# The last chunk of the modulation moved from the query stage of a hybrid attention/mLSTM step to the second half of its first group's output projection

## The chip, the cores and the metric

One core of a Trainium2 chip. The metric is the device time of one execution in microseconds; the kernel before has a median of 1595.44 us over three runs (1595.12 to 1597.05). Engines are named as in the profile: PE is TensorE, PEld its weight loads, DVE is VectorE, ACT is ScalarE, POOL is GpSimd, SP is SyncE, which here issues most DMAs.

## The reference, cut to what matters

One layer of a diffusion backbone for one prompt of 128 context tokens and one sample of 1024 latent tokens, width D = 1024, all in 32-bit floats:

```python
mods = silu(cond) @ w_ada + b_ada              # six chunks of 1024: sh1, sc1, g1, sh2, sc2, g2
h = rmsnorm(x, norm1_w) * (1 + sc1) + sh1
aq, ak, av, mq, mk, mv, mo, mg = split(h @ w_in)
attn_o = attention(rope(rmsnorm(aq)), keys, vals)       # 8 query heads, 2 key heads of 64
hm = mlstm(mq, mk, mv, gates(mg)) in both directions    # 4 heads of 128, chunks of 128
hm = rmsnorm(hm, mlstm_norm_w) * sigmoid(mo)
x = x + g1 * (concat(attn_o, hm) @ w_out)
h2 = rmsnorm(x, norm2_w) * (1 + sc2) + sh2
x = x + g2 * ((silu(h2 @ w_gate) * (h2 @ w_up)) @ w_down)   # d_ff = 2816
y = rmsnorm(x, final_norm_w)
```

The context tokens have a modulation of their own and see only themselves; the latent tokens also see the cached context keys and start their scans from given states. Outputs are y of both token groups, the new keys and values, and the final mLSTM states of the context.

## The kernel before, in words

**Tiles.** The 1152 tokens are nine blocks of 128 (block 0 is the context), in three groups of three blocks (CT = 384 tokens). A product in full precision is made of three matmuls of a high and a low part of each operand: high by high, low by high, high by low (L495 to L497 in the in-projection, L1189 to L1191 in the output projection, L1321 to L1323 in the gate and up products, L1155 to L1157 in the down product). A weight piece is loaded as 32-bit `raw`, ACT casts its high part (L152 `whi`) and DVE or POOL subtracts for the low part (`sub`, L137 `wlo`). `Scaled.pairs` (L211) does this for the scaled 16-bit pieces of the in- and output projection: by default every second piece takes one ACT step (L221) and one DVE step (L222), the others two ACT steps (L224, L225) and a DVE subtraction.

**Order of stages.** (1) Loads, the first norm, key/value/gate products and the first two chunks of the modulation. (2) The query stage: 216 query matmuls (`linear_tok` with `evac_q`), and woven in with them `gates` (the mLSTM's gate algebra), `ada` (modulation), `kwork` (norm and rotation of the keys, key stacks, values) and `steps` (the weights of head 0). (3) Four mLSTM heads: each head's projections with the scan of the head before and attention of group 0 woven in. (4) The transition: scan of head 3, output projection of group 0 (`first_out`), second norm of group 0. (5) FFN of groups 0, 1, 2, with attention and output projection of the next group woven in.

**Modulation.** `ada_rest(ns, ...)` (L422) makes the chunks named in `ns` in units of one 512 KB load of w_ada (L428, tile `a`) and four strip products (L346, which the trace shows as eight records). After four units ACT copies `part` (L446); for chunks 3 and 4 (shift and scale) PE turns it into columns (L352), for chunks 2 and 5 (the two gates) PE makes a row (L455), which is stored in `g_d` (L459). Before, `ada` makes (2, 4, 3, 5) in the query stage: 32 units in all, with three `a` buffers.

**Queries.** `evac_q` scales a block's queries out of PSUM into `qraw`, and after a pair of blocks `norm_rope` (L672) norms and rotates them and SP stores them in `q_d` (L743), from where attention loads them.

**What sets the order.** Work is written as generators. `weave(main, side, n_main, n_side)` steps `side` about n_side times over n_main steps of `main`; `beside((gen, rate), ...)` steps several generators, each by its rate; `emit` runs one to its end. `hot(n)` raises the priority of what is issued inside. From program order, priority and dependencies a scheduler then fixes each engine's queue at build time; on the chip each engine serves its own queue strictly in order. SP's queue holds loads and stores in one order, so a load behind a store waits for what that store waits for. Tiles come from pools with a fixed number of buffers per tag, and a load into a tile waits for the last reader of the buffer.

**The transition.** `first_out` (L1198) loads the rows `x1a` and the gate rows, then for each block does the attention half of the output projection (`block(0, i)`: L1218 on DVE scales the product, L1219 on POOL adds it), makes the pieces of the second half of w_out (`homes`, `spare` and `iw`), and after the mLSTM's last head does `block(1, i)` for the three blocks (addition on DVE). Then `stats` (L1280) takes the squares of the three rows on ACT (L1284) and the inverse root for all three as a chain of 12 small DVE steps (L127 to L133), the rows are copied to `cur["x1"]` by DMA (L1452), and `norm2` (L1288) per block and half scales (L1300 `y`), transposes (L116), shifts and scales (L1308, L1310 `fl`), casts (L1315 `aTh`) and subtracts (L137 `aTl`, on POOL for group 0). Attention of group 1 (scores L1075, softmax L1077 to L1082, DMA transposes L1084 and L1085, value products L1099 and L1100) is already woven in with the last scan and with norm2. Then come the first gate and up products (`gate_up`, L1325), with two `raw` buffers.

```python
weave(linear_tok(w_q, 0, 512, evac_q(qp, qcc, qss, qw)),
      beside((gates, 0.7), (ada, 1.5), (kwork, 0.6), (steps, 0.3)), 40, 40)
...
att = chain(att, attention(1, oT, set()))
weave(scan, beside((first, 0.8), (att, 0.14)), 37, 37)
```

## Time and profile before

| | us |
|---|---|
| median of three runs | 1595.44 (1595.12 to 1597.05) |
| the profiled execution | 1595.83 |
| its span | 1593.8 |
| stage of loads, key/value/gate products | 0 to 92.7 |
| query stage | 92.7 to 185.1 |
| four heads | 185.1 to 485.5 |
| transition | 485.5 to 595.4 |
| FFN of group 0, 1, 2 | 595.4 to 960, to 1320, to 1593.8 |

The stage bounds are read from the PE timeline: the first product of head 0 starts at 185.07, the last in-projection product ends at 485.5, the first gate matmul starts at 595.45. The span is the time between the first and the last recorded instruction; the execution's own time is 2.0 us longer. In the lines of the profile an instruction group is given as engine, line of the program, operation, output<-inputs, partitions x elements and a count (x24); a bracket at the end holds the idle time of the engine before it and what ended it. A line number such as L346 is that of the kernel before, printed above; helpers such as `transpose` (L116) or `sub` (L137) have one line for all their callers, so the tile names tell them apart. The granted clock is the share of TensorE's full speed that the throttle allowed.

### The profile page before, as it was taken

What the parts mean: (1) busy time and instruction counts of PE and PEld (TensorE: products, weight loads), DVE (VectorE), ACT (ScalarE), POOL (GpSimd) and SP (SyncE); (2) the same over time, 40 slices, a digit from 0 to 9 for tenths busy, and PEclk for the clock granted to TensorE, in tenths of its full rate; (3) what the DMA queues carried; (4) which work ended last, traced back from release to release, by engine and by line L of the source; (5) the groups of instructions that cost most, each with busy time, mean ns of one, the idle gap of its engine ahead of it and who ended that gap; (6) DMA issues with size and microseconds to landing.
All of it is one profiled execution on the core that took longest, in us unless ns stands there. A gap on an engine that the chain in (4) does not pass through costs nothing.

```text
span 1593.8 us, 23426 instructions
## 1 busy us (share of the span) xinstructions
PE 1494.4 (94%) x8545; PEld 1217.9 (76%) x8545; DVE 1028.1 (65%) x2047; ACT 777.6 (49%) x1448; POOL 240.9 (15%) x341
## 2 busy tenths in 40 slices
PE   6899799999997859999999999999999999999996
PEld 3544467666674549899995989989895989999995
DVE  4877624755746966878637577887856575554555
ACT  4753446846655655555331545556541443333332
POOL 0213232323233221010010101000010101001111
PEclk9899699999999889999999999999999999999998
DMA  9565503522452357978634547978763545434441
GB/s 361 179 188 181 164 11 68 114 57 64 97 130 84 67 165 182 201 159 200 180 108 119 153 138 240 192 170 179 173 152 99 151 128 183 150 124 139 146 145 53
DMA packets 384888, 230.74 MB, mean 145 GB/s; under 512 B 169894, under 2 KB 346486, under 8 KB 384774
## 3 DMA queue, kind: packets, MB, share of 16 engines
q1 hardware_dynamic: 382118, 225.68, 53.3%
q10 hardware_dynamic: 2656, 3.58, 1.0%
q8 instruction: 67, 1.10, 0.3%
q14 instruction: 47, 0.39, 0.1%
HBM read 179.39 MB, written 9.92 MB: 119 GB/s over the span
## 4 chain that ended last, share of the span: by engine, by line
PE 58%; DVE 3%; DMA 1%; ACT 0%; issue 0%; ACTq 0%
PE mm L1322 12%; PE mm L1323 12%; PE mm L1321 11%; PE mm L1155 5%; PE mm L1156 5%; PE mm L1157 4%; PE S L1075 3%; PE po L1100 1%; PE po L1099 1%; PE mm L1189 1%; PE mm L1190 1%; PE mm L1191 1%; DVE fl L1310 1%; DVE x L1145 1%; DMA plT<-pl 1%; DVE wlo L137 0%
## 5 line engine op out<-in xcount | busy, mean ns | idle before, releaser
L152 ACT CAST whi<-raw 128x1024 fp32r<-128x1024 f32 (+1 forms) x204 | 209.0, 1025 | 375.6 <-PE mm L1322 151.5
L1321 PE MATMUL mm<-aTh,whi 128*128 128x384 f32 x1056 | 354.7, 337 | 5.0 <-ACT whi L152 5.0
L1322 PE MATMUL mm<-aTl,whi 128*128 128x384 f32 x1056 | 355.8, 337 | 2.7 <-DVE aTl L137 2.7
L137 DVE TENSOR_TENSOR wlo<-raw,whi 128x1024 fp32r<-128x1024 f32 (+1 forms) x204 | 245.4, 1203 | 171.4 <-ACT whi L152 168.8
L1323 PE MATMUL mm<-aTh,wlo 128*128 128x384 f32 x1056 | 354.9, 336 | 0.0
L137 POOL TENSOR_TENSOR hl<-tn,hl 128x384 fp32r<-128x384 f32 x66 | 82.6, 1252 | 884.9 <-ACT hl L1344 772.3
L1321 PEld LDWEIGHTS mm<-aTh,whi 128*128 128x128 f32 x1056 | 198.8, 188 | 6.0 <-ACT whi L152 5.4
L1322 PEld LDWEIGHTS mm<-aTl,whi 128*128 128x128 f32 x1056 | 198.9, 188 | 3.9 <-DVE aTl L137 3.3
L1323 PEld LDWEIGHTS mm<-aTh,wlo 128*128 128x128 f32 x1056 | 199.0, 188 | 0.1
L1156 PE MATMUL mm<-wlo,hl 128*128 128x512 f32 x372 | 145.4, 391 | 0.0
L1155 PE MATMUL mm<-whi,hl 128*128 128x512 f32 x372 | 144.7, 392 | 0.0
L1157 PE MATMUL mm<-whi,hl 128*128 128x512 f32 x372 | 143.1, 392 | 0.0
L495 PE MATMUL wi<-ipair,hT 128*128 128x384 f16 (+2 forms) x408 | 135.4, 334 | 1.9 <-ACT hT L519 1.2
L496 PE MATMUL wi<-ipair,hT 128*128 128x384 f16 (+2 forms) x408 | 135.3, 334 | 0.0
L497 PE MATMUL wi<-ipair,hT 128*128 128x384 f16 (+2 forms) x408 | 131.3, 333 | 1.0 <-DVE hT L137 1.0
L1082 DVE SCALAR_TENSOR_TENSOR pl<-pr,st,ph 128x1152 f16<-128x1152 f32 (+1 forms) x72 | 94.5, 1313 | 43.1 <-ACT ph L1081 36.5
L1078 ACT ACTIVATE pr<-S,st 128x1152 f32<-128x1152 f32 (+1 forms) x72 | 81.4, 1131 | 57.1 <-DVE st L1077 45.8
L1077 DVE TENSOR_REDUCE st<-S 128x1 f32<-128x1152 f32 (+1 forms) x72 | 88.7, 1233 | 19.0 <-PE S L1075 18.8
L1081 ACT ACTIVATE ph<-pr,st 128x1152 f16<-128x1152 f32 (+1 forms) x72 | 83.9, 1165 | 27.7 <-DVE st L1080 10.6
L1075 PE MATMUL S<-kst,qT 128*128 128x384 f32 (+1 forms) x400 | 88.8, 355 | 3.0 <-ACT pr L1078 2.8
L1157 PEld LDWEIGHTS mm<-whi,hl 128*128 128x128 f32 x372 | 69.9, 188 | 14.4
L1155 PEld LDWEIGHTS mm<-whi,hl 128*128 128x128 f32 x372 | 69.9, 188 | 13.8
(390 smaller groups left out, 2524.1 us busy)
## 6 DMA issues: line engine op xcount, KB each, us to landing
raw<-in_w_gu_dram SPq DMA_DIRECT2D x132, 512.0 KB, 4.1
raw<-in_w_down_dram SPq DMA_DIRECT2D x60, 512.0 KB, 4.1
a<-in_w_ada_dram SPq DMA_DIRECT2D x32, 512.0 KB, 4.5
gl<-g_d SPq DMA_DIRECT2D x34, 256.0 KB, 4.6
aw<-in_w_ada_dram SPq DMA_DIRECT2D x16, 512.0 KB, 10.1
iraw<-in_w_in_dram SPq DMA_DIRECT2D x32, 256.0 KB, 4.1
x<-in_x_sample_dram SPq DMA_DIRECT2D x14, 512.0 KB, 5.9
iraw<-in_w_out_dram SPq DMA_DIRECT2D x8, 512.0 KB, 5.1
```

The source lines that it names most:

```text
L137: (dve if eng == "dve" else pool).tensor_tensor(out=out, in0=full, in1=hi, op=ALU.subtract)
L152: nc.scalar.copy(hi[:, :n], raw[:, :n])
L495: mm(ps[:, :n], ah, wh[:, k % 2, c0 : c0 + n], start=(k == 0), stop=False)
L496: mm(ps[:, :n], ah, wl[:, k % 2, c0 : c0 + n], start=False, stop=False)
L497: mm(ps[:, :n], al, wh[:, k % 2, c0 : c0 + n], start=False, stop=(k == KD - 1))
L1075: mm(S[:, n, 0:w], qT[:, h, :], kst[kv][:, t, c0 + n * w : c0 + (n + 1) * w], start=(t == 0), stop=(t == 1))
L1155: mm(ps, ah, wh[:, k % 2, :], start=(k == 0), stop=False)
L1156: mm(ps, ah, wl[:, k % 2, :], start=False, stop=False)
L1157: mm(ps, al, wh[:, k % 2, :], start=False, stop=(k == nk - 1))
L1321: mm(ps, wh[:, k, :], th[:, k, :], start=(k == 0), stop=False)
L1322: mm(ps, wh[:, k, :], tl[:, k, :], start=False, stop=False)
L1323: mm(ps, wl[:, k, :], th[:, k, :], start=False, stop=(k == KD - 1))
```

## The change

- `ada` in the query stage makes chunks (2, 4, 3); chunk 5 (g2, eight units, two rows) becomes `ada5`, with a pool of its own (`a5` with two buffers), stepped beside the second output half and norm2 of group 0.
- The rates beside the query matmuls and beside the heads change: n_side 12 to 10 and `ada` 1.5 to 1.15, `att` 0.11 to 0.12, in the last scan `first` 0.8 to 0.5 and `att` 0.14 to 0.1.
- Query rows are stored one pair of blocks later (`late_q`, `flush_q`), the new key and value cache rows in `value_parts`.
- Both halves of w_out take the one-ACT, one-DVE form for every piece (`pairs(1)`).
- `first_out` ends after the pieces; the loop behind it does, for each block, the second output half with its sum written straight to `cur["x1"]`, that block's statistics, and norm2 of the block before. The three copies L1452 go. `aTl` is subtracted on DVE.
- Two gate pieces (`early`) are loaded before norm2 of the third block, attention of group 1 is set up only after `first_out`, and the PSUM pools of the FFN and the pool `hlp` open at other places.

```diff
@@ -461,7 +461,7 @@
 
     es_r = ExitStack()
     adp = es_r.enter_context(tc.tile_pool(name="adp", bufs=1, side="right", reuse_waits="tile"))
-    ada = ada_rest((2, 4, 3, 5), padded_sil(adp.tile([P, KD, 32], F32, name="silp2")),
+    ada = ada_rest((2, 4, 3), padded_sil(adp.tile([P, KD, 32], F32, name="silp2")),
                    lambda: adp.tile([P, 4, 256], F32, name=nm("a4"), tag="a4", bufs=3),
                    lambda: adp.tile([P, 512], F32, name=nm("part"), tag="part", bufs=1),
                    lambda: adp.tile([2, 512], F32, name=nm("row"), tag="row", bufs=1))
@@ -525,7 +525,7 @@
             features(c)
         prods = linear_tok(kvg_pairs, 0, 272, evac_kvg, (tuple(range(c * CB, c * CB + CB)),), bank if c == 1 else bankA)
         if c > 0:
-            weave(prods, chain(steps, ada), KD, 12)
+            weave(prods, chain(steps, ada), KD, 10)
         else:
             emit(prods)
         if c == 0:
@@ -705,8 +705,6 @@
         for b in (0, 4):
             norm_rope(qp, cc, ss, kall[:, b : b + 4], 4, NKV, kw, (b, b + 4))
             yield
-        dma(O["new_cache_k"][0, 0], kall[:, 9])
-        dma(O["new_cache_v"][0, 0], vall[:, 9])
 
         vm = qp.tile([P, 4], F32, name="vm")
         dve.tensor_reduce(out=vm[:, 0:1], in_=vall, axis=AX.XYZ, op=ALU.max, apply_absolute_value=True)
@@ -727,6 +725,13 @@
         dve.tensor_copy(vsc[:, 0:2], ps[:, 0:2])
         yield
 
+    late_q = []
+
+    def flush_q():
+        for bb, rows in late_q:
+            dma(q_d[bb], rows)
+        late_q.clear()
+
     def evac_q(qp, cc, ss, qw):
         held = {}
 
@@ -739,8 +744,8 @@
             if b == grp[-1]:
                 nb = len(grp)
                 norm_rope(qp, cc, ss, qr[:, 0:nb], nb, NQ, qw, (max(grp[0], 1) - 1, grp[-1]))
-                for i, bb in enumerate(grp):
-                    dma(q_d[bb], qr[:, i].rearrange("p h d -> p (h d)"))
+                flush_q()
+                late_q.extend((bb, qr[:, i].rearrange("p h d -> p (h d)")) for i, bb in enumerate(grp))
 
         return evac
 
@@ -936,7 +941,6 @@
                         continue
                     (nc.scalar.dma_start if h == NH - 1 and c > 0 else dma)(
                         hm_d[c][:, h * 2 * P : (h + 1) * 2 * P].rearrange("(b p) n -> p b n", p=P), t.rearrange("p b t x -> p b (t x)"))
-                    yield
             yield
 
 
@@ -996,6 +1000,9 @@
 
     def value_parts():
 
+        dma(O["new_cache_k"][0, 0], kall[:, 9])
+        dma(O["new_cache_v"][0, 0], vall[:, 9])
+        yield
         for i0 in (0, 5):
             v = vall[:, i0 : i0 + 5]
             dve.tensor_scalar(out=v, in0=v, scalar1=vsc[:, 0:1], scalar2=None, op0=ALU.mult)
@@ -1012,11 +1019,12 @@
     groups_in[0].inverses()
     steps = groups_in[1].ready()
     next(steps)
-    weave(linear_tok(w_q, 0, 512, evac_q(qp, qcc, qss, qw)), beside((gates, 0.7), (ada, 1.5), (kwork, 0.6), (steps, 0.3)), 40, 40)
+    weave(linear_tok(w_q, 0, 512, evac_q(qp, qcc, qss, qw)), beside((gates, 0.7), (ada, 1.15), (kwork, 0.6), (steps, 0.3)), 40, 40)
     emit(gates)
     emit(steps)
     groups_in[1].made = groups_in[1].pairs()
     emit(ada)
+    flush_q()
     emit(kwork)
     es_r.close()
     es_h.close()
@@ -1195,7 +1203,7 @@
         nc.scalar.copy(m[:, :, 0], o)
         sub(m[:, :, 1], o, m[:, :, 0], eng)
 
-    def first_out(oT, ready, mx, hm_done):
+    def first_out(oT, ready, mx, second):
 
 
         x1 = hTp.tile([P, CB, D], F32, name="x1a", tag="hT0")
@@ -1209,16 +1217,17 @@
             dma(x1[:, i], xrow(i))
         yield
 
-        def block(half, i):
+        def block(half, i, to=None):
             for n in range(2):
                 cs = slice(n * 512, (n + 1) * 512)
                 ps = out_block(w_o[half].made, n, mx[:, half, i])
                 v = x1[:, i, cs]
                 tmp = gt[:, 4 + n]
                 dve.scalar_tensor_tensor(out=tmp, in0=ps, scalar=wos[:, half : half + 1], in1=gt[:, 2 * n + (i > 0)], op0=ALU.mult, op1=ALU.mult)
-                (pool if half == 0 else dve).tensor_tensor(out=v, in0=v, in1=tmp, op=ALU.add)
+                (pool if half == 0 else dve).tensor_tensor(out=v if to is None else to[:, cs], in0=v, in1=tmp, op=ALU.add)
                 yield
 
+        second.append(block)
         for i in range(CB):
             while i not in ready:
                 yield
@@ -1236,14 +1245,8 @@
             w = wp.tile([P, 2, 1024], F16, name=nm("iw"), tag="iraw", bufs=4)
             return w[:, 0], w[:, 1]
 
-        w_o[1].made = w_o[1].pairs(homes=homes)
+        w_o[1].made = w_o[1].pairs(1, homes)
         keep_scale(1)
-        yield
-        while 0 not in hm_done:
-            yield
-        for i in range(CB):
-            yield from block(1, i)
-        x1s.extend(x1[:, i] for i in range(CB))
 
     def keep_scale(half):
         t = w_o[half].t
@@ -1287,7 +1290,7 @@
 
     def norm2(c, a, i):
 
-        x1 = a.get("x1n", a["x1"])[i]
+        x1 = a["x1"][i]
         if "h2" not in a:
             a["h2"] = a_tiles()
         th, tl = a["h2"]
@@ -1313,7 +1316,7 @@
                         op0=ALU.mult, op1=ALU.add)
                 oh = th[:, half * 4 : half * 4 + 4, i * P : (i + 1) * P]
                 nc.scalar.copy(oh, full)
-                sub(tl[:, half * 4 : half * 4 + 4, i * P : (i + 1) * P], full, oh.bitcast(F32), "pool" if c == 0 else "dve")
+                sub(tl[:, half * 4 : half * 4 + 4, i * P : (i + 1) * P], full, oh.bitcast(F32), "dve")
             yield True
 
     def products(ps, wh, wl, th, tl):
@@ -1329,8 +1332,7 @@
             if True:
                 pg, pu = bank(), bank()
                 for off, ps in ((0, pg), (D_FF, pu)):
-                    src = w_gu[:, off + f * P : off + (f + 1) * P].rearrange("(k p) n -> p k n", p=P)
-                    wh, wl = load_piece([(full_view, src)], (KD, P))
+                    wh, wl = a["early"].pop(0) if a.get("early") else gate_piece(f, off)
                     products(ps[:, 0:CT], wh, wl, th, tl)
                     yield 6
                 parts = [(slice(0, CT), pg[:, 0:CT], pu[:, 0:CT])]
@@ -1417,48 +1419,73 @@
     weave(head_project(0, sts[0]), beside((att, 0.1),), 96, 96)
     for h in range(1, NH):
         scan = head_mlstm(h - 1, sts[h - 1])
-        weave(head_project(h, sts[h]), beside((scan, 0.42), (att, 0.11)), 96, 96)
+        weave(head_project(h, sts[h]), beside((scan, 0.42), (att, 0.12)), 96, 96)
         emit(scan)
-    x1s, hm_done = [], set()
-    w_o[0].made = w_o[0].pairs()
+    second, hm_done = [], set()
+    w_o[0].made = w_o[0].pairs(1)
     keep_scale(0)
     mx0 = hTp.tile([P, 2, CB, 4, 2, P], F16, name="mx0", tag="hT2")
     for i in range(CB):
         dma(mx0[:, 1, i, 0:3].rearrange("p k t x -> p (k t x)"), hm_d[0][i * P : (i + 1) * P, 0 : 3 * 2 * P])
-    first = first_out(oT, done, mx0, hm_done)
+    first = first_out(oT, done, mx0, second)
     scan = head_mlstm(NH - 1, sts[NH - 1], mx0[:, 1], hm_done)
-    oT = []
-    att = chain(att, attention(1, oT, set()))
-    weave(scan, beside((first, 0.8), (att, 0.14)), 37, 37)
+    weave(scan, beside((first, 0.5), (att, 0.1)), 37, 37)
     while len(done) < CB:
         next(att)
     emit(scan)
     emit(first)
+    oT = []
+    att = chain(att, attention(1, oT, set()))
     es_m.close()
+    es_d.close()
+    for name, bufs in (("mm", 4), ("po", 1)):
+        psum[name] = ctx.enter_context(tc.tile_pool(name="q" + name, bufs=bufs, space=PSUM, reuse_waits="tile"))
     ft = ctx.enter_context(tc.tile_pool(name="ft", bufs=1, side="right", reuse_waits="tile"))
     for tag, bufs in (("gl", 1), ("gx", 1), ("t2", 3)):
         ft.tile([P, 512], F32, name=f"lay_{tag}", tag=tag, bufs=bufs)
     fp = ctx.enter_context(tc.tile_pool(name="fp", bufs=1, side="right", reuse_waits="tile"))
-    hlp = ctx.enter_context(tc.tile_pool(name="hlp", bufs=1, side="right", reuse_waits="tile"))
-    hlp.tile([P, 2, CT], F32R, name="lay_hl", tag="hl", bufs=5)
+    es_x = ExitStack()
     hpr = ctx.enter_context(tc.tile_pool(name="hpr", bufs=1, side="right", reuse_waits="tile"))
 
     cur, nxt = {}, {}
     cur["x1"] = new_x1(0)
-    cur["x1n"] = x1s
-    with hot(400):
-        cur["rs"] = stats(x1s)
+    cur["rs"] = []
+
+    def gate_piece(f, off):
+        src = w_gu[:, off + f * P : off + (f + 1) * P].rearrange("(k p) n -> p k n", p=P)
+        return load_piece([(full_view, src)], (KD, P))
+
+    xp = es_x.enter_context(tc.tile_pool(name="xp", bufs=1, side="right", reuse_waits="tile"))
+    ada5 = ada_rest((5,), padded_sil(xp.tile([P, KD, 32], F32, name="silp5")),
+                    lambda: xp.tile([P, 4, 256], F32, name=nm("a5"), tag="a5", bufs=2),
+                    lambda: xp.tile([P, 512], F32, name=nm("part5"), tag="part5", bufs=1),
+                    lambda: xp.tile([2, 512], F32, name=nm("row5"), tag="row5", bufs=1))
+
+    def step5(n):
+        for _ in range(n):
+            next(ada5, None)
+
     for i in range(CB):
-        dma(cur["x1"][i], x1s[i])
-        for _ in norm2(0, cur, i):
+        for _ in second[0](1, i, cur["x1"][i]):
+            step5(2)
+        with hot(200):
+            cur["rs"] += stats(cur["x1"][i : i + 1])
+        if i > 0:
+            for _ in norm2(0, cur, i - 1):
+                step5(1)
             next(att, None)
     es1.close()
     es_wp.close()
-    es_d.close()
-    for name, bufs in (("mm", 4), ("po", 1)):
-        psum[name] = ctx.enter_context(tc.tile_pool(name="q" + name, bufs=bufs, space=PSUM, reuse_waits="tile"))
     wp = ctx.enter_context(tc.tile_pool(name="wp", bufs=1, reuse_waits="tile"))
     hpl = ctx.enter_context(tc.tile_pool(name="hpl", bufs=1, reuse_waits="tile"))
+    with hot(400):
+        cur["early"] = [gate_piece(0, 0), gate_piece(0, D_FF)]
+    for _ in norm2(0, cur, 2):
+        step5(2)
+    emit(ada5)
+    es_x.close()
+    hlp = ctx.enter_context(tc.tile_pool(name="hlp", bufs=1, side="right", reuse_waits="tile"))
+    next(att, None)
     nxt["x1"] = new_x1(1)
 
     def groups(c, a, lst):
```

## The prediction

> **What bounds the kernel now.** I read the page first: the span, the engines' busy time, and the chain that ended last.
>
> ```profile
> span 1593.8 us, 23426 instructions
> PE 1494.4 (94%) x8545; PEld 1217.9 (76%) x8545; DVE 1028.1 (65%) x2047; ACT 777.6 (49%) x1448; POOL 240.9 (15%) x341
> ```
>
> TensorE (PE) works 94% of the span and is idle for 1593.8 − 1494.4 = 99.4 us in all. The change adds no matmul, so a gain can only come out of those 99.4 us and of time at a low clock; anything that lands where PE is already full costs its own length. The busy time by stage says where that is (columns: length, then busy time of PE, PEld, DVE, ACT, POOL, then the granted clock, DMA share, GB/s).
>
> ```profile
> 92.70:156.90 64.20, 62.72 (x403) 30.04 (x400) 45.69 (x168) 28.77 (x55) 16.35 (x11) 1.00 0.63 190
> 156.90:185.10 28.20, 17.27 (x93) 7.74 (x94) 23.97 (x60) 17.33 (x37) 7.48 (x4) 0.58 0.69 214
> 140.00:185.00 45.00, 33.38 (x197) 15.64 (x196) 37.54 (x105) 26.85 (x51) 12.49 (x8) 0.74 0.66 206
> 485.50:595.40 109.90, 77.59 (x404) 52.38 (x404) 79.86 (x222) 63.11 (x150) 30.83 (x39) 0.86 0.42 111
> 595.40:960.00 364.60, 363.40 (x1988) 323.22 (x1989) 249.37 (x366) 165.23 (x219) 30.77 (x24) 0.99 0.63 161
> 960.00:1320.00 360.00, 358.04 (x1988) 316.81 (x1988) 261.79 (x390) 174.60 (x233) 25.91 (x22) 1.00 0.68 165
> ```
>
> The change touches two soft places. The first is the tail of the query stage, 156.9 to 185.1: 28.2 us with 17.3 of PE work at a clock of 0.58. The second is the transition, 485.5 to 595.4: 32 us without PE work, at 0.86. The stages behind (FFN of groups 0 and 1) have 1.2 and 2.0 us of slack in 360: what is pushed there is paid in full.
>
> The PE timeline of the tail (start, length, instruction, idle before it and what ended it):
>
> ```profile
> 156.49 0.38 PE L497 MATMUL wi<-ipair,hT 128*128 128x512 f16 x1
> 161.46 1.71 PE L352 MATMUL mm<-strip_sel,part 128*128 128x2 f32 x8 [4.59 <-ACT part L446]
> 167.18 1.12 PE L116 MATMUL mm<-ident,qr 128*128 128x128 f32 x4
> 176.16 1.08 PE L346 MATMUL mm<-a,silp 128*32 128x256 f32 x8 [1.78 <-DMA a<-in_w_ada_dram]
> 179.59 1.08 PE L346 MATMUL mm<-a,silp 128*32 128x256 f32 x8 [2.35 <-DMA a<-in_w_ada_dram]
> 181.38 1.87 PE L455 MATMUL mm<-part,strip_sel 128*2 128x512 f32 x2 [0.70 <-ACT part L446]
> 183.18 0.48 PE L116 MATMUL mm<-ident,ai 128*128 128x128 f32 x1
> 185.07 0.48 PE L827 MATMUL wi<-hT,ipair 128*128 128x384 f16 x1
> L346 PE MATMUL mm<-a,silp 128*32 128x256 f32 x64 | 9.0, 633 | 4.2 <-DMA a<-in_w_ada_dram 4.1
> a<-in_w_ada_dram SPq DMA_DIRECT2D x32, 512.0 KB, 4.5
> ```
>
> The last query product starts at 156.49 (they follow each other by about 0.2, so it is out of the way at 156.9), the first product of head 0 at 185.07. Between them stand 64 records of L346. A unit of modulation work is one 512 KB load and eight such records, so this is exactly eight units, and they are late because their loads are: PE waits for `a`, then for ACT's copy of `part`.
>
> **The change part by part.**
>
> *The modulation rows leave the query stage.* ada_rest no longer gets chunk 5, which is eight units of the 32 loads. In the order in which the changed program issues, only four L352, four gate transposes, the four `qr` transposes and the two small score matmuls remain between the last query product and head 0. At the low clock of before these take 1.71 + 1.12 + 1.9 (from the `ai` transpose at 183.18 to 185.07) = 4.7 us. The 24 other units lie among the query matmuls, as 24 of the 32 did before; by my walk along SP's queue two of their loads now come behind stores (a query group's rows, the new state) and hold PE back by about 2 us each, so the last product ends near 161. Head 0 then starts at 161 + 4.7 = 165.7. Its weight pieces and the norms of the last two query groups are DVE's, and DVE was busy 37.5 of the 45 us up to 185; I take 167. **Gain 185.1 − 167 = 18 us.** Bounds: no load wait and no DVE wait, 156.9 + 4.7 = 161.6, gain 24; all of the late DVE work stays in front of head 0, gain 3.
>
> *Query rows stored one group later, cache rows later.* These are the same stores, moved behind loads in SP's queue. They shorten the waits of loads behind them and are in the walk; by themselves 0, and if that cover fails, one load time, 4.5.
>
> *The head weights of the output projection by one ACT and one DVE step instead of ACT, ACT, DVE for every second piece.* ACT makes one pass fewer on four pieces (about 1 us each, as ACT's cast of a piece in a row below), DVE's count stays. It lies under matmuls of other lines: 0, at worst 1 us either way.
>
> *Attention of group 1 no longer starts in the last scan.* The PE timeline of the transition:
>
> ```profile
> 488.71 0.27 PE L1099 MATMUL mm<-phT,vs 128*128 128x256 f16 x1
> 490.57 0.27 PE L1100 MATMUL mm<-plT,vs 128*128 128x256 f16 x1
> 522.09 1.30 PE L1075 MATMUL S<-kst,qT 128*128 128x384 f32 x6
> 534.53 2.29 PE L1075 MATMUL S<-kst,qT 128*128 128x384 f32 x6 [0.76 <-ACT pr L1078]
> 541.09 2.29 PE L1075 MATMUL S<-kst,qT 128*128 128x384 f32 x6 [0.92 <-ACT pr L1078]
> 551.14 0.38 PE L1189 MATMUL mm<-spare,mx 128*128 128x512 f16 x1
> 576.52 1.11 PE L116 MATMUL mm<-ident,y 128*128 128x128 f32 x4 [8.73 <-ACT y L1300]
> 595.45 0.69 PE L1321 MATMUL mm<-aTh,whi 128*128 128x384 f32 x1 [5.05 <-ACT whi L152]
> L1075 PE MATMUL S<-kst,qT 128*128 128x384 f32 x42 | 11.1, 409 | 1.7 <-ACT pr L1078 1.7
> ```
>
> Before, seven score steps (42 matmuls of L1075) and two value products of group 1 are done ahead of the first gate matmul (595.45). The changed order holds three score steps and no value product there. So four score steps at 1.30 (full clock, the 522.09 row) and two value products at 490.57 + 0.27 − 488.71 = 2.1, less the overlap of the last, 2.0, move into the FFN of group 0: 4 × 1.30 + 2 × 2.0 = **9.2 us, paid there**, since PE has 1.2 us of slack in it. Bounds: 8.0, if that slack is used, and 9.2.
>
> *What is left of the scan.* Five of the score steps stood between 522 and 548 in the scan; with their waits they took 1.30 + 1.3 + 3.05 + 3.21 + 1.3 = 10.2. Without them the second output half can start at 551.14 − 9.4 = 541.7 (0.8 kept back, as the scan has steps of its own to wait for). Bounds 539 and 545.
>
> *Second output half block by block, with chunk 5, statistics and norms.* The rows for it:
>
> ```profile
> 573.38 0.17 DVE L127 TENSOR_SCALAR rv<-s 128x3 f32<-128x3 f32 x1 [3.79 <-ACT jk L1284]
> 575.55 0.16 DVE L133 SCALAR_TENSOR_TENSOR ry<-rt,ry 128x3 f32<-128x3 f32 x1
> 575.75 1.33 ACT L1300 ACTIVATE y<-x1a,ry 128x512 f32<-128x512 f32 x2 [2.41 <-DVE ry L133]
> 594.36 1.04 ACT L152 CAST whi<-raw 128x1024 fp32r<-128x1024 f32 x1
> 595.88 1.22 DVE L137 TENSOR_TENSOR wlo<-raw,whi 128x1024 fp32r<-128x1024 f32 x1
> raw<-in_w_gu_dram SPq DMA_DIRECT2D x132, 512.0 KB, 4.1
> 590.76 3.05 SPq L1084 DMA_TRANSPOSE phT<-ph  x1
> 571.75 2.02 SPq L1452 DMA_DIRECT2D x<-x1a  x3
> 580.66 1.27 POOL L137 TENSOR_TENSOR aTl<-fl,aTh 128x512 fp32r<-128x512 f32 x1 [17.39 <-ACT aTh L1315]
> ```
>
> Before, PE stood for 8.73 us while the statistics of all three blocks were made. That wait should go: two blocks' statistics now lie beside the third block's products. What is late next is the chain in ACT's queue. With two buffers of `a` and a load of 4.5 us, eight units come at about 3.1 us each, two every 6.2: unit 4 is done 12.3 us after the start T0, unit 8 at 25. ACT's copies of `part` wait for these in order, and `y` of the second block stands behind the second copy: T0 + 25.7. The square of the third block follows at 28.4, the first gate piece's cast at 30.4. Then the order has the casts of the third and fourth gate piece *ahead* of `y` of the third block, and the raw pieces have two buffers: each waits for a DVE subtraction (1.22) and a load (4.1), 5.3 us, two of them 10.6: `y` at T0 + 41. Four transposes, the scale and shift steps, the casts, twice, and one more piece's cast take some 6.4. First gate matmul: 541.7 + 47.4 = 589.1, against 595.45: **gain 6.4**. Bounds: if the ring doesn't hold ACT, 10.6 earlier, 578.5, gain 17; if the loads stand behind two issues on SP like the transpose of 3.05, six later, gain 0.
>
> The three copies of x1a into x go, and they were issued inside the 8.73 us wait; the subtraction `aTl` (1.27 on POOL, six of them) goes to DVE, which is busy 79.9 of 109.9 us there; the 1-column rsqrt comes three times instead of once (575.7 − 573.4 = 2.3 us each, two of them beside products): these are in the chain above.
>
> One rule speaks against the earlier start. The rows first:
>
> ```profile
> 528.34 2.22 DVE L222 SCALAR_TENSOR_TENSOR spare<-iraw,isc,spare 128x1024 f16<-128x1024 f32 x1
> 537.14 1.28 DVE L222 SCALAR_TENSOR_TENSOR iw<-iraw,isc,iw 128x1024 f16<-128x1024 f32 x1
> 528.21 1.27 POOL L1219 TENSOR_TENSOR x1a<-x1a,gta 128x512 f32<-128x512 f32 x1 [3.57 <-DVE st L1080]
> ```
>
> The same DVE step took 2.22 us while POOL's addition ran and 1.28 without it. The Trainium skill, "GPSIMD Engine Reference", section "1. Specifications", says that POOL shares its SBUF interfaces with VectorE and contends with DVE instructions that have two SBUF inputs; this pair of rows agrees. The changed order puts three such additions beside four L222 steps: by the rule T0 comes up to 3 × 0.94 = 2.8 us later, by the sum 0; I leave the sum as it is.
>
> **Sum**, against the profiled execution's own time, 1595.83 us (the span of 1593.8 and 2.0 around it; the median of the three runs is 1595.44, 0.4 lower): 1595.8 − 18 − 6.4 + 9.2 = 1580.6.
>
> **The rivals.**
>
> A. *The ring of gate pieces does not hold up `y`.* If ACT reaches `y` of the third block before the refilled pieces, the first gate matmul is at 578.5: 1595.8 − 18 − 17 + 9.2 = 1570. For: the issue order is the scheduler's, and if the third block's rows are ready early the 10.6 us shrink. Against: ACT serves its queue in order, and the later casts stand ahead.
>
> B. *SP holds the loads of the transition.* Gate pieces, rows of chunk 5 and attention's transposes share SP's queue. Two issues of 3.05 us, six us: first gate matmul at 595, gain of the transition 0: 1595.8 − 18 + 9.2 = 1587.
>
> C. *Slower: DVE sets the start of head 0.* The norms and rotations of the last query groups, the weight pieces and the key work are DVE work that the change leaves as it is. If they end where they did, PE waits for them instead of for `a`, and the gain of the query stage is 0 to 3. With the transition's gain lost to SP as in B, the 9.2 us of displaced attention stay: 1595.8 − 3 + 9.2 = 1602 at most, and 1599 with half of the transition's gain. It decides from about 182 on: if head 0 starts later than that, the kernel is slower. For it: DVE's 37.5 of 45 us. Against: in the tail itself DVE is busy 24 of 28 us and part of that is work of chunk 5 and of waiting groups that can come earlier, beside the query products, where DVE has 45.7 of 64.2.
>
> D. *The change doesn't do what it says.* The eight units find no idle time in the transition and stand on PE's path there as they did in the query stage: their 4.2 us of load waits and 4 us of matmuls come back. The transition then takes as long as before and some 8 us more: 1595.8 − 18 + 9.2 + 8 = 1595, no change.
>
> **How the numbers follow.** Forecast 0.45 (its own range 1574 to 1587), A 0.12, B 0.18, C 0.17, D 0.08. A measurement of this kernel can tell about 0.2%, 3.2 us. Forecast, A and B are faster by more than that: 0.75; D is split between the same (0.05) and slower or faster by a little; C is slower but for 0.01. So faster 0.76, same 0.06, slower 0.18. The range is from 1565, which is A with five of the six us that the query stage's upper bound adds, to 1600, which holds D and half of C; outside it lie about 0.08 above and 0.07 below. The time is the forecast's, rounded to 1581.
>
> **What would show it.** Query stage: no L346 between the last L497 and head 0's first product, which starts at 165 to 169; a start beyond 182 speaks for C, with a DVE step as releaser. Transition: no wait of 8 us for `y` of the first block; T0 near 542; ACT's casts of the third and fourth piece ahead of the third block's `y`; the first gate matmul 6 us earlier in distance from the last head's products (485.5) than the 110 of before, 99 for A, 110 for B. FFN of group 0: longer by 8 to 9 us, the others as they were. The forecast is wrong if head 0 starts beyond 175, if FFN of group 0 keeps its 364.6 us, or if the transition gets longer.

## The result, and the profile after

The changed kernel takes 1587.53 us (median of four runs, 1585.00 to 1588.74) against 1595.28 for the kernel before (four runs beside it): ratio 0.9948, 95% interval 0.9931 to 0.9965. The profiled execution took 1588.74, 7.1 less than that of before. A second measurement of the same changed kernel beside the last experiments gave 1585.55 and a ratio of 0.9923 (0.9910 to 0.9936). The kernel before had medians of 1595.3 to 1598.3 in the different sessions, so what follows compares ratios, and stages within profiles.

The page of the changed kernel:

```profile
span 1586.9 us, 23427 instructions
PE 1493.5 (94%) x8545; PEld 1214.6 (77%) x8545; DVE 1033.8 (65%) x2078; ACT 774.7 (49%) x1444; POOL 231.6 (15%) x336
```

PE's work is the same (1493.5 against 1494.4), its idle time 93.4 instead of 99.4. The busy time by stage, first of the changed kernel, then of the kernel before where its stage had not been shown as one (length; busy PE, PEld, DVE, ACT, POOL; clock, DMA share, GB/s):

```profile
92.70:166.50 73.80, 68.52 (x417) 31.66 (x415) 56.96 (x196) 38.88 (x77) 16.64 (x11) 0.98 0.55 164
166.50:469.60 303.10, 290.27 (x1868) 204.62 (x1868) 167.63 (x448) 185.44 (x525) 93.45 (x204) 0.98 0.37 79
469.60:528.30 58.70, 40.47 (x206) 26.25 (x205) 44.27 (x147) 33.23 (x104) 22.00 (x34) 0.87 0.26 79
528.30:579.40 51.10, 35.94 (x188) 17.68 (x187) 35.33 (x89) 23.18 (x38) 0.00 (x0) 0.77 0.68 197
579.40:937.40 358.00, 357.23 (x1970) 316.00 (x1969) 244.83 (x356) 166.08 (x219) 28.16 (x22) 0.99 0.64 157
```

```profile
185.10:485.50 300.40, 287.34 (x1843) 201.63 (x1842) 158.75 (x420) 183.61 (x519) 84.85 (x201) 0.99 0.34 74
485.50:551.10 65.60, 49.21 (x254) 35.11 (x255) 49.14 (x135) 41.57 (x108) 19.24 (x27) 0.84 0.32 79
551.10:595.40 44.30, 28.38 (x151) 17.27 (x149) 30.73 (x88) 21.55 (x42) 11.59 (x12) 0.88 0.57 157
595.40:945.20 349.80, 349.63 (x1909) 309.76 (x1910) 235.06 (x336) 158.09 (x208) 30.77 (x24) 0.99 0.63 160
```

The transition is cut at the first product of the second output half, and FFN of group 0 ends here at the first gate matmul of group 1 (945.2 and 937.4), so that both kernels are cut at the same instruction. The ledger, before to after:

| stage | before | after | difference | forecast |
|---|---|---|---|---|
| up to head 0 | 185.1 | 166.5 | −18.6 | −18 |
| four heads | 300.4 | 303.1 | +2.7 | 0 |
| transition, to the second output half | 65.6 | 58.7 | −6.9 | −9.4 |
| transition, from there to the first gate matmul | 44.3 | 51.1 | +6.8 | +3.1 |
| FFN of group 0 | 349.8 | 358.0 | +8.2 | +9.2 |
| the rest of the span | 648.6 | 649.5 | +0.9 | 0 |
| sum | 1593.8 | 1586.9 | −6.9 | −15.1 |

The two transition terms of the forecast are 56.2 (541.7 − 485.5) and 47.4. **The transition gave nothing**: it starts its second half 6.9 us sooner and loses that again.

In the PE timeline of the changed kernel the query stage's tail has no L346; the first product of head 0, the fourth unit of chunk 5 (L346) and the transition's longest waits are these:

```profile
166.47 0.32 PE L832 MATMUL wi<-hT,ipair 128*128 128x384 f16 x1 [1.27 <-DVE QT L668]
527.59 0.90 PE L116 MATMUL mm<-ident,hmc 128*128 128x128 f32 x3 [6.75 <-POOL hmc L928]
541.90 0.64 PE L346 MATMUL mm<-a,silp 128*32 128x256 f32 x8
573.08 1.97 PE L116 MATMUL mm<-ident,y 128*128 128x128 f32 x8 [9.67 <-ACT y L1303]
```

The wait of 8.73 us for `y` of the first block has shrunk to 1.38; in its place stand a wait of 6.75 for the head's last scaling on POOL and one of 9.67 for `y` of the *third* block. ACT's timeline says why the latter:

```profile
542.66 0.58 ACT L446 COPY part<-mm 128x512 f32<-128x512 f32 x1 [4.52 <-PE mm L346]
556.66 0.58 ACT L446 COPY part<-mm 128x512 f32<-128x512 f32 x1 [6.68 <-PE mm L346]
557.14 1.33 ACT L1303 ACTIVATE y<-x,ry 128x512 f32<-128x512 f32 x2
568.53 1.04 ACT L152 CAST whi<-raw 128x1024 fp32r<-128x1024 f32 x1 [3.07 <-DMA raw<-in_w_gu_dram]
571.35 1.04 ACT L152 CAST whi<-raw 128x1024 fp32r<-128x1024 f32 x1 [1.77 <-DMA raw<-in_w_gu_dram]
572.30 1.33 ACT L1303 ACTIVATE y<-x,ry 128x512 f32<-128x512 f32 x2
```

ACT waits for the fourth and eighth unit of chunk 5 (L446), and then `y` of the third block stands behind the casts of the third and fourth gate piece, each of which waits for its load.

### The profile page after: what moved, and what is told of

Same layout as the page of the kernel before. It is cut to its first block, busy times and chain, and to the rows that moved or that the text cites. A ratio compares the mean times of both kernels' runs of the same rounds, so it can differ in the third digit from the quotient of the medians.

```text
span 1586.9 us, 23427 instructions
## 1 busy us (share of the span) xinstructions
PE 1493.5 (94%) x8545; PEld 1214.6 (77%) x8545; DVE 1033.8 (65%) x2078; ACT 774.7 (49%) x1444; POOL 231.6 (15%) x336
## 4 chain that ended last, share of the span: by engine, by line
PE 60%; DVE 4%; DMA 2%; ACT 1%; issue 0%; SPq 0%; DVEq 0%; ACTq 0%
PE mm L1325 12%; PE mm L1326 12%; PE mm L1324 11%; PE mm L1163 4%; PE mm L1164 4%; PE mm L1165 4%; PE S L1083 3%; PE mm L1197 2%; PE mm L1198 2%; PE mm L1199 2%; PE po L1107 2%; PE po L1108 2%; DVE fl L1313 1%; DVE x L1153 1%; DVE wlo L137 1%; DMA raw<-in_w_gu_dram 1%
## 5 line engine op out<-in xcount | busy, mean ns | idle before, releaser
L137 DVE TENSOR_TENSOR wlo<-raw,whi 128x1024 fp32r<-128x1024 f32 (+1 forms) x204 | 244.9, 1200 | 163.8 <-ACT whi L152 163.2
L1165 PEld LDWEIGHTS mm<-whi,hl 128*128 128x128 f32 x372 | 69.9, 188 | 14.3
L1164 PEld LDWEIGHTS mm<-wlo,hl 128*128 128x128 f32 x372 | 69.9, 188 | 13.8
```

Of the source, the lines that this page charges most:

```text
L137: (dve if eng == "dve" else pool).tensor_tensor(out=out, in0=full, in1=hi, op=ALU.subtract)
L1164: mm(ps, ah, wl[:, k % 2, :], start=False, stop=False)
L1165: mm(ps, al, wh[:, k % 2, :], start=False, stop=(k == nk - 1))
```

## The experiments

The theory is the forecast's: the query tail is chunk 5's waiting for loads; the displaced attention is paid in FFN of group 0; the transition is held by chunk 5's loads and by the casts ahead of `y`. The rivals stand with each run; labels such as e4 are those that the quoted expectations use. Times are medians; each ratio is to the kernel before on the same chip, with its 95% interval.

**Chunk 5 back in the query stage (e1).**

```diff
-    ada = ada_rest((2, 4, 3), ...
+    ada = ada_rest((2, 4, 3, 5), ...      # n_side 12 and rate 1.5 as before
-    ada5 = ada_rest((5,), ...
+    ada5 = iter(())
```

> The changed kernel with chunk 5 back in the query stage (rates 1.5 and 12 as before), nothing beside the second output half. If the gain is the query stage's tail: head 0 starts near 185 instead of 166.5 (18.6 us lost), the transition is some 5 us shorter since ACT's copies of part no longer stand ahead of y: about 1601, slower than both kernels. Rival, that the gain comes from the late query stores and the rates: head 0 starts below 172 and the time stays at 1587 to 1592.

1593.67 us, 0.9981 (0.9971 to 0.9991). Its stages, up to head 0, and the two parts of the transition:

```profile
92.70:184.90 92.20, 79.11 (x495) 37.03 (x494) 69.72 (x227) 46.06 (x91) 24.14 (x15) 0.90 0.64 197
484.40:542.50 58.10, 40.23 (x205) 26.16 (x204) 44.31 (x147) 33.23 (x104) 21.92 (x33) 0.88 0.24 71
542.50:585.60 43.10, 27.75 (x120) 15.96 (x119) 31.94 (x85) 21.16 (x35) 0.00 (x0) 0.78 0.41 116
```

Head 0 is back at 184.9, so the tail is chunk 5's. The late stores stayed in this run and don't make it; the rates went back together with the units that they pace and are not told apart from them. But the second part of the transition falls from 51.1 to 43.1: chunk 5 costs 8.0 there. The price was forecast at 5, so the total missed (1601 was expected): moving chunk 5 is worth 18.4 − 8.0 less 3.6, by which the heads are longer in the changed kernel (299.5 here), and less some 3 us in smaller differences: the spans are 1590.7 here and 1586.9 in the changed kernel.

**The product of chunk 5 left out (e3)** (its two rows hold only the bias, so y is not the reference's; the units' loads, strips and copies are gone).

> The changed kernel with the product of chunk 5 left out (its two rows hold only the bias). If the eight units hold up the transition through ACT's copies of part (4.5 and 6.7 us of waiting there), the distance from the last head product to the first gate matmul falls from 110 to 102 to 104, and the time to about 1580. Rival, that they are hidden beside the output half: distance 108 to 110, time 1585 to 1587.

1577.28 us, 0.9877 (0.9863 to 0.9891). The part from the second output half to the first gate matmul:

```profile
526.40:569.30 42.90, 27.43 (x119) 15.90 (x118) 32.15 (x85) 20.98 (x35) 0.00 (x0) 0.78 0.45 129
```

42.9, as in the run before it: 8.2 us less than with chunk 5, and 101.7 from the last head product to the first gate matmul, where 102 to 104 was expected. Chunk 5 is not hidden beside the output half; that rival falls.

But the records do not show ACT's copies of `part` holding the transition up. These are the groups on PE between the second output half's first product and the first gate matmul, in the changed kernel and then, for `y` alone, with chunk 5 back in the query stage:

```profile
L346 PE MATMUL mm<-a,silp 128*32 128x256 f32 x64 | 4.9, 390 | 0.8 <-DMA a<-in_w_ada_dram 0.8
L455 PE MATMUL mm<-part,strip_sel 128*2 128x512 f32 x4 | 2.9, 813 | 0.0
L116 PE MATMUL mm<-ident,y 128*128 128x128 f32 x24 | 5.2, 381 | 12.4 <-ACT y L1303 12.4
```

```profile
L116 PE MATMUL mm<-ident,y 128*128 128x128 f32 x24 | 4.4, 333 | 12.6 <-ACT y L1303 12.6
```

PE waits for `y` as long without chunk 5 as with it (12.6, and 11.9 with the product left out, against 12.4), and it is idle as long (15.4 and 15.5 us against 15.2). What goes is busy time: 8.2 and 8.5 us of it, of which the units' own matmuls are 4.9 + 2.9 = 7.8. PE waited only 0.8 us for the loads `a`. So chunk 5 costs here what its matmuls cost on PE.

**Attention of group 1 set up early again (e4).**

```diff
+    oT = []
+    att = chain(att, attention(1, oT, set()))
-    weave(scan, beside((first, 0.5), (att, 0.1)), 37, 37)
+    weave(scan, beside((first, 0.5), (att, 0.14)), 37, 37)
...
-    oT = []
-    att = chain(att, attention(1, oT, set()))
     es_m.close()
```

> The changed kernel with attention of group 1 again set up before the last scan, at the rate 0.14 of before. If the 8.4 us lost in FFN of group 0 are the displaced score and value steps, that stage gets 5 to 9 us shorter; the scan and the transition get longer, by about as much (the five steps took 10 us with their waits before): 1585 to 1590. Rival, that the displacement is a plain loss because the transition has idle time for them: 1579 to 1581. Rival, that FFN of group 0 lost time for another reason: that stage stays and the total is up by 5 or more.

1585.75 us, 0.9927 (0.9915 to 0.9940). The two parts of the transition, and FFN of group 0:

```profile
468.50:539.30 70.80, 49.75 (x257) 33.72 (x256) 56.29 (x166) 42.75 (x118) 22.24 (x34) 0.86 0.40 102
539.30:586.10 46.80, 35.18 (x197) 17.22 (x194) 32.33 (x89) 22.81 (x38) 0.00 (x0) 0.83 0.64 188
586.10:934.00 347.90, 347.65 (x1910) 307.25 (x1910) 233.49 (x337) 156.59 (x206) 28.98 (x22) 1.00 0.62 157
```

FFN of group 0 falls by 10.1 us, the transition grows by 7.8 (70.8 + 46.8 = 117.6 against 109.8). The ratio lies between the two of the changed kernel: whether these steps stand in the one stage or the other makes no difference that can be told from none. That the displacement is a plain loss falls too.

**No early gate pieces (e6).**

```diff
-    with hot(400):
-        cur["early"] = [gate_piece(0, 0), gate_piece(0, D_FF)]
```

> The changed kernel without the two gate pieces made ahead of the third block's norm2. In its issue order y of the third block stands before the casts of the third and fourth piece. If these casts, waiting for their loads, hold up y (PE waited 9.67 us for it), that wait falls to 3 to 5 us and the first gate matmul comes 4 to 6 us earlier: about 1582. Rival, that y waits for its own statistics on DVE or that the pieces are then late themselves: 1586 to 1590, with a wait for whi before the first gate matmul.

1582.63 us, 0.9911 (0.9898 to 0.9925). The second part of the transition, and in ACT's timeline `y` of the third block:

```profile
527.30:575.80 48.50, 35.84 (x187) 17.47 (x186) 32.99 (x86) 22.54 (x38) 0.00 (x0) 0.78 0.65 186
```

```profile
566.02 1.04 ACT L152 CAST whi<-raw 128x1024 fp32r<-128x1024 f32 x1 [0.52 <-DMA raw<-in_w_gu_dram]
568.62 1.33 ACT L1303 ACTIVATE y<-x,ry 128x512 f32<-128x512 f32 x2 [1.56 <-DVE ry L133]
```

The casts were part of it: 48.5 instead of 51.1 (51.5 to 52.2 in e2, e7, e9 and the second profile of the changed kernel), and `y` starts 41.3 us after the second output half's start instead of 44.0. But the wait for `y` fell only from 9.67 to 7.0, not to 3 to 5: now `y` waits for `ry`, its own inverse root, whose steps stand between others in DVE's queue. In the changed kernel that root ended at 571.1 and the fourth piece's cast at 572.4: the cast was the last to hold `y`, but the root was ready only 1.3 us before it, and that the forecast hadn't reckoned with.

**Query rows stored at once (e2); attention of group 0 at 0.11 (e7).** Two small parts undone, each alone.

```diff
-                flush_q()
-                late_q.extend(...)
+                for i, bb in enumerate(grp):
+                    dma(q_d[bb], qr[:, i].rearrange("p h d -> p (h d)"))
```

> The changed kernel with the query rows stored at once, as before. If moving the eight units alone makes the earlier start of head 0, it starts at 165 to 169 and the time stays within 2 us of the changed kernel's (ratio 0.994 to 0.996 to the kernel before). Rival, that the stores stood in front of the loads and the late stores are part of the gain: head 0 3 to 8 us later, ratio 0.997 to 1.0.

1584.17 us, 0.9927 (0.9914 to 0.9940), head 0 at 164.0: the late stores bring nothing that can be told. Head 0 starts at 163.7 to 164.7 in the three runs that store at once, and at 163.8 to 166.5 in the nine that store late with chunk 5 out of the query stage, so this start varies by more than 2 us between runs.

```diff
-        weave(head_project(h, sts[h]), beside((scan, 0.42), (att, 0.12)), 96, 96)
+        weave(head_project(h, sts[h]), beside((scan, 0.42), (att, 0.11)), 96, 96)
```

> The changed kernel with attention of group 0 at the rate 0.11 beside the heads, as before. If the 2.8 us that the four heads got longer are the two value products pulled into them by 0.12, the heads take 299 to 300.5 us instead of 303 and the transition 1 to 4 more (they then stand where PE is idle in part): total 0 to 3 us less than the changed kernel. Rival, that the heads got longer for another reason (a low clock or waits after the earlier start): they stay at 303.

1586.30 us, 0.9938 (0.9925 to 0.9951). The four heads, and the transition:

```profile
166.30:465.80 299.50, 285.83 (x1845) 201.80 (x1844) 168.69 (x446) 185.82 (x529) 94.44 (x203) 0.99 0.37 80
465.80:577.60 111.80, 77.11 (x412) 43.87 (x413) 79.06 (x236) 55.24 (x139) 23.79 (x35) 0.83 0.43 130
```

The heads are 3.6 shorter and the transition 2.0 longer. So the rate 0.12 had pulled the last two value products of group 0 into the heads. The groups of L1107, the value products in the heads, show it as 76 matmuls in the changed kernel against 58 here (and 58 in the kernel before):

```profile
L1107 PE MATMUL mm<-phT,vs 128*128 128x256 f16 x76 | 18.9, 288 | 0.5 <-DVE sd L861 0.3 <-ACT cs L820 0.2
```

```profile
L1107 PE MATMUL mm<-phT,vs 128*128 128x256 f16 x58 | 13.2, 273 | 0.0
```

**Additions of the first output half on DVE (e9).**

```diff
-                (pool if half == 0 else dve).tensor_tensor(out=v if to is None else to[:, cs], ...
+                dve.tensor_tensor(out=v if to is None else to[:, cs], ...
```

> The changed kernel with the additions of the first output half on DVE (L1227) instead of POOL. In the changed kernel DVE steps of 0.16 us took 1.12 and 1.26, and one L222 1.94 instead of 1.28, while POOL added, and the head's scaling on POOL (L928) stood behind the additions. If that puts off the second output half (6.75 us of PE waiting for L928), it starts 2 to 4 us sooner after the last head, 55 to 57 instead of 58.6, and the time falls by 2 to 3. Rival, that DVE's own queue is the limit there: same start, as DVE has three more steps of 0.7, and the same time.

1583.37 us, 0.9915 (0.9903 to 0.9927). The first part of the transition:

```profile
467.70:525.10 57.40, 40.31 (x205) 26.20 (x204) 45.01 (x153) 32.83 (x104) 14.01 (x28) 0.88 0.27 81
```

57.4 instead of 58.7, and PE's wait for L928 5.9 instead of 6.8: the direction of the theory, but less than the 2 to 4 us that it gave. The step is small but repeats: this part takes 57.4 to 57.7 in the three profiles with these additions on DVE and attention of group 1 set up late (e9, e13, e14), and 58.1 to 59.2 in seven with the additions on POOL. L928 itself took 0.83 us instead of the 1.81 that it took beside an L222 of DVE; the rest of PE's wait stays, since POOL now waits for the root that L928 needs, on DVE. The ratio's interval overlaps that of the changed kernel's second measurement.

**Three buffers for chunk 5's loads (e12).** The changed kernel was measured again beside it.

```diff
-                    lambda: xp.tile([P, 4, 256], F32, name=nm("a5"), tag="a5", bufs=2),
-                    lambda: xp.tile([P, 512], F32, name=nm("part5"), tag="part5", bufs=1),
-                    lambda: xp.tile([2, 512], F32, name=nm("row5"), tag="row5", bufs=1))
+                    lambda: xp.tile([P, 4, 256], F32, name=nm("a5"), tag="a5", bufs=3),
+                    lambda: ft.tile([P, 512], F32, name=nm("t2"), tag="t2", bufs=3),
+                    lambda: xp.tile([2, 512], F32, name=nm("row5"), tag="row5", bufs=1), 3)
```

> The changed kernel itself once more, beside the next three on one chip, so that steps of 2 to 5 us can be compared with it: ratio 0.993 to 0.9965 to the kernel before, the stages within 1 us of its first profile (head 0 at 166.5, transition 109.7, first group's FFN 358.1) if these bounds are the program's own; head 0 at 164 if the 2 us between runs at that place are the chip's.

> The changed kernel with three buffers for the loads of chunk 5 in the transition instead of two (the copies of part in a tile of the FFN's pool). If the loads set the pace of the eight units (3 us a unit) and their copies on ACT put off y, the fourth unit ends 10 to 12 us after the second output half's start instead of 14, and the first gate matmul comes 2 to 4 us earlier: time 2 to 4 below the changed kernel's. Rival, that the units stand where the issue order puts them and the third block's chain decides: within 1 us of the changed kernel.

The changed kernel again: 1585.55, 0.9923 (0.9910 to 0.9936). With three buffers: 1581.88, 0.9899 (0.9883 to 0.9915). The second part of the transition, of the one and of the other:

```profile
526.90:578.40 51.50, 35.87 (x187) 17.57 (x186) 35.22 (x89) 23.19 (x38) 0.00 (x0) 0.77 0.67 194
```

```profile
525.90:573.40 47.50, 34.12 (x188) 16.39 (x186) 33.53 (x86) 22.35 (x38) 0.00 (x0) 0.82 0.63 178
```

4.0 us less, but not because the units came faster. The fourth unit still ends 14.2 us after the second output half's start, not 10 to 12, and the eighth after 27.8 instead of 28.3. On PE the fourth unit, and on ACT the steps around the second copy (its tile is `t` here), of the run with three buffers:

```profile
539.49 0.64 PE L346 MATMUL mm<-a,silp 128*32 128x256 f32 x8
```

```profile
552.78 1.33 ACT L1303 ACTIVATE y<-x,ry 128x512 f32<-128x512 f32 x2 [5.04 <-DVE ry L133]
556.95 0.58 ACT L446 COPY t<-mm 128x512 f32<-128x512 f32 x1
566.07 1.33 ACT L1303 ACTIVATE y<-x,ry 128x512 f32<-128x512 f32 x2 [4.12 <-DVE ry L133]
568.68 1.04 ACT L152 CAST whi<-raw 128x1024 fp32r<-128x1024 f32 x1 [1.28 <-DMA raw<-in_w_gu_dram]
```

The order in ACT's queue is another: `y` of the second block stands ahead of the second copy of `part`, and `y` of the third ahead of the third gate piece's cast, and each waits only for its inverse root. So the rival is right that the units stand where the issue order puts them, and wrong that the time stays. The edit does two things at once (a third buffer with loads one unit further ahead, and more room for the copies of `part`); which of them gave the other order was not tried.

The changed kernel's own stages repeat to 1.5 us (head 0 at 166.1, heads 302.0, transition 58.8 and 51.5, FFN of group 0 356.6).

**Together (e10, e13, e14).** Three combinations: early attention, no early pieces and additions on DVE; then stores at once, no early pieces and additions on DVE; then the latter with the third buffer.

> Early attention of group 1 (as e4), no early gate pieces (as e6), additions on DVE (as e9) in one kernel. If the three act at separate places, their gains add: 3 + 6 + 2 = 11 us below the changed kernel, ratio 0.988 to the kernel before. Rival, that early attention already uses the time that PE waited for y: 5 to 7 below, ratio 0.991.

> The changed kernel with stores at once (e2), no early gate pieces (e6) and the additions on DVE (e9). If e6 and e9 act at separate places and the stores cost nothing: 5 to 8 us below the changed kernel, ratio 0.989 to 0.9905. Rival, that the earlier start of the second output half only lengthens the wait for y: same as e6, ratio 0.991.

> As the run before it, with the three buffers of e12 too. If both theories hold: 7 to 11 us below the changed kernel, ratio 0.987 to 0.9895. Rival: as without the third buffer.

1581.61, 0.9907 (0.9894 to 0.9920): the rival's ratio, so the three gains don't add, and early attention adds nothing to the other two, as alone. 1582.32, 0.9906 (0.9890 to 0.9923): 3.2 below the changed kernel beside it, less than the 5 to 8 expected. And **1576.04, 0.9867 (0.9852 to 0.9883)**, 9.5 below, which beats both kernels; the second part of its transition:

```profile
524.20:568.80 44.60, 35.79 (x188) 16.34 (x185) 32.32 (x88) 21.24 (x37) 0.00 (x0) 0.84 0.63 183
```

6.9 less than the 51.5 of the changed kernel beside it, with all of chunk 5 still in it: PE is busy as long (35.8) and idle 8.8 us instead of 15.6. By the total alone, no other run with the whole product and chunk 5 in the transition is clear of both intervals of the changed kernel; those readings rest on the stages.

## Why the prediction was right, and where its sum was off

The direction held and the time lay in the range, 6.5 us above the forecast. By its steps:

- *The modulation rows leave the query stage* (gain 18): right, 18.6. Head 0 at 166.47 (forecast 167), and the wait before it is short and DVE's. That it came so close is luck in part: the last query product started at 163.1 and not near 161, and the rest took 3.4 us and not 6. Chunk 5 put back returned the tail (184.9); rival C, DVE as the bound, falls with it.
- *Query rows stored later, 0*: right; undone alone, no difference that can be told.
- *Attention displaced, 9.2, paid in FFN of group 0*: right, 8.2 and 6.8 in the two profiles. The steps are the ones counted: the groups of that stage, changed kernel, then before, have 25 score matmuls and 18 of L1107 more.

```profile
L1083 PE MATMUL S<-kst,qT 128*128 128x384 f32 x127 | 26.7, 344 | 0.0
L1107 PE MATMUL po<-phT,vs 128*128 128x256 f16 x108 | 25.4, 274 | 0.0
```

```profile
L1075 PE MATMUL S<-kst,qT 128*128 128x384 f32 x102 | 22.0, 353 | 0.1
L1099 PE MATMUL po<-phT,vs 128*128 128x256 f16 x90 | 21.4, 276 | 0.0
```

- *The weights by one ACT and one DVE step, 0*: not tried alone.
- *The transition, gain 6.4*: **the term that was mis-sized**; it measured 0.1. T0, the start of the second output half, came 2.5 later (58.7 for 56.2), since the last scaling of the head waits on POOL and DVE; in e7, where two value products stand in this part again, it took 59.8. From T0 it took 51.1 for 47.4. The forecast's order on ACT was right: second copy of `part`, `y` of the second block, square, four casts, `y` of the third block. But `y` of the second block already started 28.8 us after T0 instead of 25.7; from there to `y` of the third block it took 15.2, forecast 15.3. So the step that failed is the pace of the eight units. The forecast took it from their loads (3.1 us each, the fourth done at 12.3 and the eighth at 25) and put their matmuls on PE at nothing. They were done at 14.2 and 28.3 with 0.8 us of waiting for loads, and until then PE was busy 25.8 of 28.3 us, 5.9 of them with chunk 5:

```profile
528.30:556.60 28.30, 25.79 (x157) 10.54 (x155) 19.69 (x52) 7.48 (x14) 0.00 (x0) 0.96 0.48 143
```

- *The rate of attention beside the heads* had no term. The heads got 2.7 longer; undoing the rate took 3.6 from them and put 2.0 into the transition.

Of the rivals, B came closest in time (1587): the transition's gain was lost. Its mechanism, issues on SP in front of the loads, is small here: the load of the fourth gate piece was issued at 567.30 behind a transpose, 0.5 us after its buffer came free. D is nearer to what happened: the eight units stand on PE's path in the transition and cost its 8 us, though as 7.8 of matmuls and 0.8 of waiting, not 4 and 4.2. Its total of 1595 didn't come, because the transition without chunk 5 is 8.7 shorter than before (58.1 + 43.1 = 101.2 against 109.9, in the run with chunk 5 back), and chunk 5 used that up. The transition's 0.1 is so the difference of two larger terms.

What stays open: why ACT's queue is ordered otherwise with three buffers, and why the heads took 299.5 in the run with chunk 5 back, with the same 76 value products, against 301.2 to 304.0 in the eleven other profiles at the rate 0.12. With chunk 5 back PE was busy 287.8 us in the heads, against 290.3 in the changed kernel's first profile for the same work, at a granted clock of 0.99 against 0.98; no run was made for the reason.

## What to carry to other kernels

Work that is moved out of a stage where it waits must be priced again where it lands, first by its own instructions on the engine that is busy there: here 18.6 us were won and 8 paid back, as long as PE took for the moved matmuls, while their loads were in time. The waits beside it are another matter: a run in which ACT's queue had `y` ahead of the copies and casts got 4 us back with the same matmuls. Where a stage behind is full, deferring work into it is only a transfer; look for who gains before counting it. After a wait has been removed, follow the queue of the engine that ended it one step further, on each engine that it passes: `y` had casts in front of it, and an inverse root that was ready only 1.3 us before the last of them.

## What the runs showed of the hardware

Small steps of DVE stretched to the end of a POOL addition that they met. In the changed kernel, on DVE and on POOL:

```profile
517.27 1.12 DVE L129 TENSOR_SCALAR ry<-rh 128x3 int32<-128x3 int32 x1
521.03 1.26 DVE L133 SCALAR_TENSOR_TENSOR ry<-rt,ry 128x3 f32<-128x3 f32 x1
524.91 1.94 DVE L222 SCALAR_TENSOR_TENSOR iw<-iraw,isc,iw 128x1024 f16<-128x1024 f32 x1
```

```profile
517.10 1.27 POOL L1227 TENSOR_TENSOR x1a<-x1a,gta 128x512 f32<-128x512 f32 x1
521.00 1.26 POOL L1227 TENSOR_TENSOR x1a<-x1a,gta 128x512 f32<-128x512 f32 x1 [2.64 <-DVE rt L132]
524.50 1.26 POOL L1227 TENSOR_TENSOR x1a<-x1a,gta 128x512 f32<-128x512 f32 x1 [2.24 <-DVE ry L133]
```

With the additions on DVE the same L129 took 0.17:

```profile
515.54 0.17 DVE L129 TENSOR_SCALAR ry<-rh 128x3 int32<-128x3 int32 x1
```

The three steps lost about 2.7 us. The sum took 0, and T0 came 2.5 later; of this, moving the additions gave back 1.3. The loss is near the 2.8 that the forecast had set beside its sum by the rule of the Trainium skill, "GPSIMD Engine Reference", section "1. Specifications", on the SBUF interfaces that POOL shares with VectorE. But the 2.8 were for three L222 steps, and only one of the four met an addition; the two small steps made up the rest. Each of the two small steps ends within 0.03 us of the addition that it met (517.27 + 1.12 and 517.10 + 1.27). The Trainium skill, "SBUF — State Buffer", section "SBUF: two separate sides", says that the pair of ports that VectorE and GpSimd share is held by one of them for a whole instruction and not split; these rows agree, since an operation on three elements a partition loses as much as what is left of POOL's step.
